# One rotation table for the S5 mixer, a weight ring opened earlier, and lane transfers moved from SyncE's queue to POOL's and ScalarE's in a hybrid decoder block

## The chip, the cores and the metric

The kernel runs on one core of a Trainium2 chip. The metric is the device time of one execution in microseconds (us). The engines are called PE (TensorE, matrix products), DVE (VectorE), ACT (ScalarE), POOL (GpSimd) and SP (SyncE, which here only issues transfers).

## The reference

One decoder block in float32, on 1024 tokens and 16 meta tokens in front of them (1040 positions), width 1024:

```python
h = LN0(concat(meta, x))
p = h @ w_in + b_in            # u_s5 512 | q 512 | k 512 | v 1024 | o 1024 | i 4 | f 4 | g_s5 1024 | g_m 1024
y_s5 = GLU(GELU(S5(u_s5)))     # per group: x_t = Abar x_{t-1} + Bbar u_t (complex, 64 states), y_t = Re(C x_t) + D u_t
y_m  = (sigmoid(o) * HeadNorm(mLSTM(q, k, v, i, f))) @ m_w_out      # 4 heads, chunkwise
mix  = sigmoid(g_s5) * y_s5 + sigmoid(g_m) * y_m
h = LN1(ALPHA * h + mix @ w_o)
h = LN2(ALPHA * h + relu(h @ w_up + b_up)**2 @ w_down)
```

The meta positions are dropped at the end.

## The kernel before, in words

**Products.** Each float32 operand of the large products is split into a rounded part ("hi", written by ACT) and a remainder ("lo", written by DVE), and each product is the sum of three matmuls (`mm3`, L226 to L228). A weight tile is loaded into `wraw`, ACT writes `whi` (L212, or L1042 in the gates), DVE writes `wlo` (L213 or L1043), and PE reads both. Some products are done by a scheme of seven half-size products in place of eight (`Seven`, and the up and down projections); it needs sums of weight blocks and of input blocks.

**Stages.** First the layer norm of h with the first q and k products in an order written out by hand. Then a list of jobs in the order of `ORDER`: `q`, `v`, `o`, `u`, `g` (g_s5), `m` (the first two of g_m), and after it eight `z` jobs (the GLU products). A job takes one weight tile through all columns of h. Then the other six tiles of g_m and m_w_out in the scheme of seven (`gates_and_output`), then w_o with LN1, the up projection and the down projection with LN2.

**Lanes.** Beside the jobs run generators, called lanes: `cv` (convolution of q and k), `ml` (gate rows and mLSTM, head after head), `s5c` (constants of the S5 mixer), `s5` (its four batches of 8 groups), `s5g` (GELU), `ah` (scaled residual and weight sums of the first three pairs of the up projection). After every two terms of a product `pump` advances an estimated clock, and each lane whose due time has come emits its next piece. The yields are these due times. The `s5` lane waits until the constants of its batch are there, and an `o` job drives the `ml` lane until its head is ready.

**Order.** The instructions so emitted pass through a scheduler that simulates the engines and fixes the order of each engine's and each queue's instructions; earlier emitted ones go first where they are ready, and weight splits have a raised priority. On the chip each queue is then in order: an instruction that waits holds all behind it. `tc.keep_in_program_order` pins some transfers to the order of emission.

**Memory.** Nearly all large tiles come from one pool of 30 slots of 128 x 1056 floats (`slot`). A tile gets its slot when the last reader of the slot's former tile has ended. Small tiles of the first stages lie in the pool `mid`. When `mid` is closed, a pool `ring` of three 128 x 1024 tiles takes its place, for the weight tiles of `gates_and_output`.

**S5.** The recurrence is run on blocks of 8 positions: 130 blocks, a real scan with decay r8 after rotation by a unit complex number p8 to the power of the block number. `s5_pre` makes Abar, its powers E, r8 and p8. `s5_consts(b)` makes for batch b the matrices Mi, RS and Mx and the table T, the cosines and sines of the powers 0 to 129 of p8 for the batch's four columns, by eight doublings of six DVE operations (`cmul`, L572 to L577) on the scratch tile `s5tt`. `s5_batch(b)` reads u from DRAM (`u_load`, L786), multiplies (tile `s5Z`), rotates, scans, rotates back, and writes y (L863). `s5_gelu(b)` reads y in another layout (`s5yc`, L871) and writes `gelh` and `gell` (L877, L878), which the z jobs read.

**Around the seam from z7 to the gates.** `begin` issues eight loads of h (`rawb`, L991), `first` then loads three weight tiles (L1024), splits the first and forms block differences. The products n = 1 and 2 use blocks of h as they lie in hT; from n = 6 on, changed blocks are written over them.

**Weight sums.** `w_sums` has POOL issue 16 transfers from DRAM to DRAM, some adding on the way, each behind a copy of one element (`mark`, L972) that waits for the weight split of the current job.

**Transfers.** All lane transfers but those into Mx and the weight sums are issued by SP, in one queue with the weight loads.

Of the kernel before, what the change touches and what calls it, by code (L numbers as in the profile page):

```python
# [40 lines left out]
ORDER = "q0 q1 v0 q2 v1 q3 o1 o0 v2 o2 o3 u0 u1 v3 u2 g0 u3 g1 o4 o5 o7 o6 g2 g3 g5 g6 g4 g7 m0 m1"  # L41
S5_START = "u0"
NM = 2
# [69 lines left out]
def decoder_block(  # L113
# [80 lines left out]
    def load_w(job):  # L194
        job.raw = []
        for src, n in job.loads:
            r = slot("wraw") if ring[0] is None else ring[0].tile([P, 1024], F32, tag="wr", bufs=3, name="wraw")
            nc.sync.dma_start(r[:, :n], src)
            job.raw.append(r)
# [111 lines left out]
    def v_job(h):  # L311
# [53 lines left out]
    def gates():  # L365
        with ExitStack() as gc:
# [43 lines left out]
            v_.tensor_tensor_scan(gg, one, a, mp, op0=OP.add, op1=OP.max)  # L410
            nc.sync.dma_start(grow_dr, gg)
            wi = gt("lf2")
            a_.activation(wi, gg, AF.Exp, scale=-1.0, bias=mp)
            nc.sync.dma_start(wrow_dr, wi)
            em = gt("fr2")
# [9 lines left out]
    def bcast_row(dst, src, h):  # L425
        nc.sync.dma_start(dst[:, 0:META], bass.AP(tensor=src.tensor, offset=src.offset + h * P,
                                                  ap=[[0, P], [1, META]]))
        nc.sync.dma_start(dst[:, META:LEN].rearrange("p (c s) -> p c s", s=P),
                          bass.AP(tensor=src.tensor, offset=src.offset + (4 + h) * P,
                                  ap=[[0, P], [4 * P, NCH - 1], [1, P]]))  # L430
# [104 lines left out]
    def u_job(i):  # L535
        st = {}

        def evac(bi, c0, c1, ps):
            if bi == 0:
                st["u"] = slot("uT")  # L540
            o = st["u"][:, :LEN].rearrange("p (j c) -> p c j", j=8)
            a_.activation(o[:, c0 // 8:c1 // 8, :], ps.rearrange("p (c j) -> p c j", j=8), AF.Identity,
                          bias=bft[:, JU + i:JU + i + 1])

        def done():
            nc.sync.dma_start(us_dr[i * P:(i + 1) * P].rearrange("p j c -> p (j c)"), st["u"][:, :LEN])
# [32 lines left out]
    def s5_pre():  # L579
        def t16(name):  # L580
            return mid.tile([P, 16], F32, name="s5_" + name)
        lam = mid.tile([P, 112], F32, tag="row", bufs=1, name="s5_lam")[:, :48].rearrange("p (a b) -> p a b", a=3)
        nc.sync.dma_start(lam, s5l)
        bc = slot("s5bc")
        nc.sync.dma_start(bc[:, 0:512], s5b)
        nc.sync.dma_start(bc[:, 512:1024], s5c)
        S5["bc"] = bc
        dtl = mid.tile([32, 16], F32, name="s5_d")
        nc.sync.dma_start(dtl, s5d)
        S5["d"] = dtl  # L590
# [72 lines left out]
        def v3(ap):  # L663
# [5 lines left out]
             v3(tm[:, 0:256]), v3(tm[:, 256:512]))  # L669
        yield 1.3  # L670

    GEL = {}

    def s5_consts(b):
# [85 lines left out]
        yield K5[b]  # L760
        T = slot("s5T")
        tc_, ts_ = (T[:, i * 520:(i + 1) * 520].rearrange("p (q c) -> p q c", q=4) for i in range(2))
        tmp = slot("s5tt")
        g_.memset(tc_[:, :, 0], 1.0)
        g_.memset(ts_[:, :, 0], 0.0)
        g_.tensor_copy(tc_[:, :, 1], S5["p8"][:, 0, q0:q0 + 4])
        g_.tensor_copy(ts_[:, :, 1], S5["p8"][:, 1, q0:q0 + 4])
        yield C5[b]
        n = 1
        while n < 129:  # L770
            m = min(n, 129 - n)
            sh = [P, 4, m]
            w1 = tmp[:, 0:4 * m].rearrange("p (q c) -> p q c", q=4)
            w2 = tmp[:, 512:512 + 4 * m].rearrange("p (q c) -> p q c", q=4)
            cmul(v_, tc_[:, :, n + 1:n + 1 + m], ts_[:, :, n + 1:n + 1 + m], tc_[:, :, 1:m + 1], ts_[:, :, 1:m + 1],
                 tc_[:, :, n:n + 1].to_broadcast(sh), ts_[:, :, n:n + 1].to_broadcast(sh), w1, w2)
            n *= 2
            yield C5[b]
        S5["m", b] = (RS, Mi, Mx, T)

    def u_load(b):
        U = slot("s5U")
        uv = U[:, :8 * NB].rearrange("p (g c) -> p g c", g=8)
        for j in range(8):
            src = us_dr[b * P:(b + 1) * P, j, :].rearrange("(g h) c -> h g c", h=16)
            nc.sync.dma_start(uv[16 * j:16 * j + 16], src)  # L786
        S5["u", b] = U
        return U

    def s5_batch(b):  # L790
# [60 lines left out]
        for hf in range(2):  # L851
# [10 lines left out]
            yield Y5[b]  # L862
        nc.sync.dma_start(ys_dr[b].rearrange("p g c -> p (g c)"), Y[:, 0:1024])  # L863
        lanes["s5g"].add(s5_gelu(b))

    def s5_gelu(b):
        yield 3.0
        yc = slot("s5yc")
        for g in range(8):
            src = ys_dr[b, :, (g % 2) * 4 + g // 2, :].rearrange("(t h) c -> h t c", h=16)  # L870
            nc.sync.dma_start(yc[16 * g:16 * g + 16, 0:1024].rearrange("p (t c) -> p t c", t=8), src)  # L871
# [6 lines left out]
        v_.tensor_tensor(lo[:, 0:1024], gf[:, 0:1024], f32(hi[:, 0:1024]), op=OP.subtract)  # L878
        GEL[b] = (hi, lo)
        yield 2.6  # L880
# [3 lines left out]
    def o_job(f):  # L884
        def evac(bi, c0, c1, ps):
            if bi == 0:
                o_job.s = slot("osig")
            a_.activation(o_job.s[:, c0:c1], ps, AF.Sigmoid, bias=bft[:, JO + f:JO + f + 1])
            v_.tensor_tensor(HM[f][:, c0:c1], HM[f][:, c0:c1], o_job.s[:, c0:c1], op=OP.mult)

        def done():
            nc.sync.dma_start(hm_dr[f], HM.pop(f)[:, :D])
        fm_job(JO + f, HALF, META, evac, done)
# [64 lines left out]
    def w_sums():  # L958
        todo = {}
        for s, (n0, p0, w, i0) in enumerate(((3, 0, wf, JGM + NM), (4, 3, wmo, 0))):  # L960
            def src(r, kh):
                return bass.AP(tensor=w.tensor, offset=w.offset + (i0 + r) * KT * P * P + 512 * kh,
                               ap=[[2 * KT * P * P, n0], [KT * P, P], [1, 512]])
            a11, a12, a21, a22 = src(0, 0), src(0, 1), src(1, 0), src(1, 1)
            d = [ws_dr[p0:p0 + n0, i] for i in range(4)]
            todo[s] = [(d[0], a21, 0), (d[2], a11, 0), (d[0], a22, 1), (d[2], a21, 1), (d[1], d[0], 0), (d[1], a11, 1),
# [37 lines left out]
    class Seven:  # L1004
# [138 lines left out]
    def gates_and_output():  # L1143
# [46 lines left out]
        return begin, first, run  # L1190

# [177 lines left out]
    def ah_scale():  # L1369
        gb = [slot("gB0"), slot("bB0")]  # L1370
        for i in range(2):
            nc.sync.dma_start(gb[i][:, :D], row_bcast(ln0r, D, i * D))
        rs = {}
        for t in range(9):
            if t < 8:
                rs[t] = slot("ahr")
                nc.sync.dma_start(rs[t][:, :D], ah0_dr[t * P:(t + 1) * P, :])
            if t == 0:
# [9 lines left out]
            nc.sync.dma_start(ah_dr[(t - 1) * P:t * P, :], r[:, :D])  # L1388

# [10 lines left out]
    def up_early():  # L1400
        for p in range(PRE):
            r = [slot("wur"), slot("wur")]
            for j in range(2):
                nc.sync.dma_start(r[j][:, :D], wup[2 * p + j].rearrange("p k f -> p (k f)"))
            yield 3.0
# [3 lines left out]
            for n, w in ((1, a11), (2, a12), (3, n2[:, 0:512]), (4, a22), (5, n1[:, 0:512]), (6, n1[:, 512:1024]),  # L1409
# [3 lines left out]
                v_.tensor_tensor(o[:, 512:1024], w, f32(o[:, 0:512]), op=OP.subtract)  # L1413
                nc.sync.dma_start(wu_dr[p, n - 1], f32(o[:, 0:1024]))
                yield 0.9
# [662 lines left out]
```

## Time and profile before

| | |
|---|---|
| median of 3 runs | 1566.78 us (1564.85 to 1566.83) |
| profiled execution | 1566.04 us, span 1564.2 us |
| mean granted clock of TensorE | 0.984 |
| busy share of the span | PE 97%, DVE 69%, ACT 41%, POOL 7% |
| DMA | 261.32 MB, mean 167 GB/s |

The span runs from the first to the last instruction. The profile has the busy time of each engine, the time an engine was idle before an instruction and what released it (a wait), and the clock that PE was granted. Times in the views are us from the start of the span. PE's share is that of the matmuls; an in-order engine that waits is idle. Names in the views are those of the program's tiles, "out<-in".

### The profile page before, as it was taken

Reading aid. Unit: us, or ns where it says so; the run is one execution under the profiler, and the core shown is the slowest. Engines: PE = TensorE matmul, PEld = TensorE weight load, DVE = VectorE, ACT = ScalarE, POOL = GpSimd, SP = SyncE. Lnnn points to the kernel's source line nnn. Section 1 sums busy time; section 2 is a strip of 40 time slices with the busy share of each in tenths; the row PEclk is TensorE's granted clock in tenths of the full one; section 3 lists DMA queues with packets and bytes.
Section 4 is the critical chain, followed back from the end, with each engine's and each line's share of the span. In section 5 each row is a group of like instructions: output and inputs, shape, how many; then the busy total and the mean of one; then the engine's idle time right before and its main releaser. Section 6 shows DMA issues by size and latency. Waiting matters only on the chain.

```text
span 1564.2 us, 20543 instructions
## 1 busy us (share of the span) xinstructions
PE 1515.8 (97%) x7593; PEld 1278.7 (82%) x7593; DVE 1079.9 (69%) x2083; ACT 642.7 (41%) x982; POOL 102.2 (7%) x195
## 2 busy tenths in 40 slices
PE   8999999998999998989999999999999999999997
PEld 8998988996878886768788887888888888888886
DVE  7667555659867845677789675666666679766786
ACT  6523353333355433325534324444444534433340
POOL 0000001124031200000000001000000000000000
PEclk9999999998999999989999999999999999999999
DMA  8412324414354556775353328644443798667642
GB/s 311 159 57 61 100 62 129 122 37 112 104 129 103 164 182 218 279 269 195 108 170 114 108 76 247 225 158 149 147 149 123 248 363 322 230 229 236 216 166 108
DMA packets 137509, 261.32 MB, mean 167 GB/s; under 512 B 30768, under 2 KB 52984, under 8 KB 137352
## 3 DMA queue, kind: packets, MB, share of 16 engines
q1 hardware_dynamic: 111344, 233.00, 43.7%
q0 software_dynamic: 26064, 27.01, 7.1%
q8 instruction: 60, 0.98, 0.3%
q14 instruction: 41, 0.34, 0.1%
HBM read 188.78 MB, written 84.55 MB: 175 GB/s over the span
## 4 chain that ended last, share of the span: by engine, by line
PE 31%; issue 23%; DMA 3%; DVE 2%; ACT 0%; SPq 0%; POOL 0%; POOLq 0%; DVEq 0%
PE mm L228 7%; PE mm L227 7%; PE mm L226 7%; PE sd L227 3%; PE sd L226 3%; PE sd L228 3%; DMA wpre<-wu_dr 1%; DMA rawb<-h_dr 1%; DMA wu_dr<-wpre 1%; DMA wur<-in_wup_dram 0%; DVE wlo L1043 0%; DVE wlo L213 0%; DMA woraw<-in_wo_dram 0%; POOL wpre L1621 0%; SPq L991 0%
## 5 line engine op out<-in xcount | busy, mean ns | idle before, releaser
L226 PE MATMUL mm<-hT_hi,whi 128*128 128x512 f32 (+3 forms) x604 | 231.0, 382 | 8.0 <-ACT whi L1042 5.4
L228 PE MATMUL mm<-hT_hi,wlo 128*128 128x512 f32 (+3 forms) x604 | 226.7, 380 | 5.7 <-DVE wlo L213 3.7
L227 PE MATMUL mm<-hT_lo,whi 128*128 128x512 f32 (+3 forms) x604 | 229.1, 379 | 0.0
L226 PEld LDWEIGHTS mm<-hT_hi,whi 128*128 128x128 f32 x604 | 115.7, 192 | 26.6 <-ACT whi L1042 6.2
L228 PEld LDWEIGHTS mm<-hT_hi,wlo 128*128 128x128 f32 x604 | 115.0, 191 | 25.5 <-DVE wlo L213 4.3
L227 PEld LDWEIGHTS mm<-hT_lo,whi 128*128 128x128 f32 x604 | 115.6, 191 | 17.6 <-issue 0.4
L227 PE MATMUL sd<-dwl,dah 128*128 128x512 f32 x240 | 94.5, 394 | 0.0
L228 PE MATMUL sd<-dwh,dal 128*128 128x512 f32 x240 | 94.4, 394 | 0.0
L226 PE MATMUL sd<-dwh,dah 128*128 128x512 f32 x240 | 94.2, 393 | 0.0
L1773 ACT ACTIVATE dah<-da 128x1024 fp32r<-128x1024 f32 x56 | 58.7, 1052 | 86.2 <-PE sd L227 38.9
L1777 ACT ACTIVATE dwh<-wdr 128x1024 fp32r<-128x1024 f32 x56 | 58.9, 1053 | 84.0 <-DMA wdr<-in_wdn_dram 27.5
L1774 DVE TENSOR_TENSOR dal<-da,dah 128x1024 fp32r<-128x1024 f32 x56 | 68.2, 1219 | 23.8 <-ACT dah L1773 23.3
L228 PE MATMUL mm<-dwh,dal 128*128 128x512 f32 (+1 forms) x224 | 84.5, 378 | 0.0
L226 PE MATMUL mm<-dwh,dah 128*128 128x512 f32 (+1 forms) x224 | 84.4, 377 | 0.0
L227 PE MATMUL mm<-dwl,dah 128*128 128x512 f32 (+1 forms) x224 | 84.3, 377 | 0.0
L1778 DVE TENSOR_TENSOR dwl<-wdr,dwh 128x1024 fp32r<-128x1024 f32 x56 | 68.2, 1219 | 13.1 <-ACT dwh L1777 12.4
L226 PE MATMUL mm<-whi,hT_hi 128*128 128x256 f32 (+1 forms) x256 | 75.2, 294 | 0.0
L228 PE MATMUL mm<-whi,hT_lo 128*128 128x256 f32 (+1 forms) x256 | 74.7, 292 | 0.0
L227 PE MATMUL mm<-wlo,hT_hi 128*128 128x256 f32 (+1 forms) x256 | 73.8, 288 | 0.0
L213 DVE TENSOR_TENSOR wlo<-wraw,whi 128x1024 fp32r<-128x1024 f32 (+1 forms) x46 | 56.1, 1222 | 19.1 <-ACT whi L212 18.6
L228 PE MATMUL mm<-th,wul 128*128 128x512 f32 x156 | 61.6, 395 | 0.0
L227 PE MATMUL mm<-tl,wuh 128*128 128x512 f32 x156 | 61.5, 394 | 0.0
(474 smaller groups left out, 3703.1 us busy)
## 6 DMA issues: line engine op xcount, KB each, us to landing
da<-act_dr SPq DMA_DIRECT2D x56, 512.0 KB, 5.4
wdr<-in_wdn_dram SPq DMA_DIRECT2D x56, 512.0 KB, 6.3
wur<-in_wup_dram SPq DMA_DIRECT2D x32, 512.0 KB, 4.3
act_dr<-upy SPq DMA_DIRECT2D x64, 256.0 KB, 2.5
wraw<-in_wf_dram SPq DMA_DIRECT2D x30, 512.0 KB, 6.9
wu_dr<-wpre SPq DMA_DIRECT2D x21, 512.0 KB, 4.7
wpre<-wu_dr POOLq DMA_DIRECT2D x21, 512.0 KB, 5.0
act_dr<-upx SPq DMA_DIRECT2D x32, 256.0 KB, 2.8
```

The source lines that it names most:

```text
L213: todo.append(lambda e=v_, r=r, hi=hi, lo=lo, n=n: e.tensor_tensor(lo[:, :n], r[:, :n], f32(hi[:, :n]), op=OP.subtract))
L226: t_.matmul(ps, ah, bh, start=(i == 0 and part[0]), stop=False, skip_group_check=skip)
L227: t_.matmul(ps, ah, bl, start=False, stop=False, skip_group_check=skip)
L228: t_.matmul(ps, al, bh, start=False, stop=(i == n - 1 and part[1]), skip_group_check=skip)
L1773: a_.activation(ah[:, :D], a[:, :D], AF.Copy)
L1774: v_.tensor_tensor(alo[:, :D], a[:, :D], f32(ah[:, :D]), op=OP.subtract)
L1777: a_.activation(wh, raw[i], AF.Copy)
L1778: v_.tensor_tensor(wl, raw[i], f32(wh), op=OP.subtract)
```

## The change

1. **One rotation table.** A new generator `s5_table` in the lane `s5c`, right behind `s5_pre`, makes the powers 0 to 65 of p8 for all 16 columns at once, in a tile of its own in `mid`, by seven rounds of `cmul`. In each batch ACT copies the batch's four columns of it into T, and one `cmul` on 4 x 64 elements makes the powers 66 to 129. `S5_START` is `o2` instead of `u0`, so `s5_pre` is emitted two jobs earlier.
2. **Ring.** `mid` is closed and the ring opened before z4 instead of z7; it has four buffers instead of three. The first three weight tiles of the gates are loaded before z6 (`early`), ahead of `begin`, instead of in `first` behind it. The jobs' own weight tiles all come from `slot`.
3. **Weight sums.** In the access patterns of the transfers of `w_sums` the 128 rows are the outermost dimension, and the 3 or 4 tiles the next.
4. **Issuers.** The transfers of bias rows, gate rows, broadcasts, S5 constants, U, yc, hm, the scaled residual and the early weight sums are issued by POOL (`g_`) instead of SP; those of wrow, u and y by ACT (`a_`).
5. The space set aside for POOL's transfer descriptors is 4096 instead of its default.

```diff
-S5_START = "u0"
+S5_START = "o2"
...
-            r = slot("wraw") if ring[0] is None else ring[0].tile([P, 1024], F32, tag="wr", bufs=3, name="wraw")
+            r = slot("wraw")
...
-            nc.sync.dma_start(bvt, row_bcast(bv, DV, h * DV))
+            g_.dma_start(bvt, row_bcast(bv, DV, h * DV))
...
-            nc.sync.dma_start(grow_dr, gg)
+            g_.dma_start(grow_dr, gg)
...
-            nc.sync.dma_start(wrow_dr, wi)
+            a_.dma_start(wrow_dr, wi)
...
-        nc.sync.dma_start(dst[:, 0:META], bass.AP(tensor=src.tensor, offset=src.offset + h * P,
+        g_.dma_start(dst[:, 0:META], bass.AP(tensor=src.tensor, offset=src.offset + h * P,
...
-            nc.sync.dma_start(us_dr[i * P:(i + 1) * P].rearrange("p j c -> p (j c)"), st["u"][:, :LEN])
+            a_.dma_start(us_dr[i * P:(i + 1) * P].rearrange("p j c -> p (j c)"), st["u"][:, :LEN])
...
+    def s5_table():
+        S5["T"] = T = mid.tile([P, 2, 16, 66], F32, name="s5_T")
+        tm, (c, s) = slot("s5tt"), (T[:, 0], T[:, 1])
+        g_.memset(c[:, :, 0], 1.0)
+        g_.memset(s[:, :, 0], 0.0)
+        g_.tensor_copy(c[:, :, 1], S5["p8"][:, 0])
+        g_.tensor_copy(s[:, :, 1], S5["p8"][:, 1])
+        yield 1.3
+        n = 1
+        while n < 65:
+            m = min(n, 65 - n)
+            sh = [P, 16, m]
+            cmul(v_, c[:, :, n + 1:n + 1 + m], s[:, :, n + 1:n + 1 + m], c[:, :, 1:m + 1], s[:, :, 1:m + 1],
+                 c[:, :, n:n + 1].to_broadcast(sh), s[:, :, n:n + 1].to_broadcast(sh),
+                 *(tm[:, i * 512:i * 512 + 16 * m].rearrange("p (q c) -> p q c", q=16) for i in range(2)))
+            n *= 2
+            yield 1.3
...
-        g_.memset(tc_[:, :, 0], 1.0)
-        g_.memset(ts_[:, :, 0], 0.0)
-        g_.tensor_copy(tc_[:, :, 1], S5["p8"][:, 0, q0:q0 + 4])
-        g_.tensor_copy(ts_[:, :, 1], S5["p8"][:, 1, q0:q0 + 4])
+        a_.activation(tc_[:, :, 0:66], t1, AF.Copy)
+        a_.activation(ts_[:, :, 0:66], s1, AF.Copy)
+        sh = [P, 4, 64]
+        cmul(v_, tc_[:, :, 66:130], ts_[:, :, 66:130], t1[:, :, 2:66], s1[:, :, 2:66],
+             t1[:, :, 64:65].to_broadcast(sh), s1[:, :, 64:65].to_broadcast(sh),
+             *(tmp[:, i * 512:i * 512 + 256].rearrange("p (q c) -> p q c", q=4) for i in range(2)))
         yield C5[b]
-        n = 1
-        while n < 129:
-            m = min(n, 129 - n)
...
-            nc.sync.dma_start(uv[16 * j:16 * j + 16], src)
+            g_.dma_start(uv[16 * j:16 * j + 16], src)
...
-        nc.sync.dma_start(ys_dr[b].rearrange("p g c -> p (g c)"), Y[:, 0:1024])
+        a_.dma_start(ys_dr[b].rearrange("p g c -> p (g c)"), Y[:, 0:1024])
...
-            nc.sync.dma_start(yc[16 * g:16 * g + 16, 0:1024].rearrange("p (t c) -> p t c", t=8), src)
+            g_.dma_start(yc[16 * g:16 * g + 16, 0:1024].rearrange("p (t c) -> p t c", t=8), src)
...
-                               ap=[[2 * KT * P * P, n0], [KT * P, P], [1, 512]])
+                               ap=[[KT * P, P], [2 * KT * P * P, n0], [1, 512]])
...
-            d = [ws_dr[p0:p0 + n0, i] for i in range(4)]
+            d = [ws_dr[p0:p0 + n0, i].rearrange("n p c -> p n c") for i in range(4)]
...
-            r = ring[0].tile([P, 1024], F32, tag="wr", bufs=3, name="wraw")
+            r = ring[0].tile([P, 1024], F32, tag="wr", bufs=4, name="wraw")
...
-        def first():
+        def early():
             for i in range(3):
                 g.load(i)
+
+        def first():
             g.split(0)
...
+            lanes["s5c"].add(s5_table())
...
-        if j.tag == "z7":
+        if j.tag == "z4":
             mid_ctx.close()
             ring_ctx = ExitStack()
             ring[0] = ring_ctx.enter_context(tc.tile_pool(name="ring", bufs=1, side="left"))
+        if j.tag == "z6":
+            early()
+        if j.tag == "z7":
             begin()
...
-    nc = _bacc.Bacc("TRN2", target_bir_lowering=False, num_devices=1)
+    nc = _bacc.Bacc("TRN2", target_bir_lowering=False, num_devices=1, dynamic_dma_scratch_size=4096)
```

In the same way as the lines shown, `g_` takes the place of `nc.sync` in the second transfer of `bcast_row`, the four of `s5_pre`, that of hm in `o_job`, and all of `ah_scale` and `up_early`.

More of the change, by code (lines that the diff above doesn't have):

```diff
@@ L425, in bcast_row @@
     def bcast_row(dst, src, h):
-        nc.sync.dma_start(dst[:, 0:META], bass.AP(tensor=src.tensor, offset=src.offset + h * P,
+        g_.dma_start(dst[:, 0:META], bass.AP(tensor=src.tensor, offset=src.offset + h * P,
                                                   ap=[[0, P], [1, META]]))
-        nc.sync.dma_start(dst[:, META:LEN].rearrange("p (c s) -> p c s", s=P),
+        g_.dma_start(dst[:, META:LEN].rearrange("p (c s) -> p c s", s=P),
                           bass.AP(tensor=src.tensor, offset=src.offset + (4 + h) * P,
@@ L582, in s5_pre @@
         lam = mid.tile([P, 112], F32, tag="row", bufs=1, name="s5_lam")[:, :48].rearrange("p (a b) -> p a b", a=3)
-        nc.sync.dma_start(lam, s5l)
+        g_.dma_start(lam, s5l)
         bc = slot("s5bc")
-        nc.sync.dma_start(bc[:, 0:512], s5b)
-        nc.sync.dma_start(bc[:, 512:1024], s5c)
+        g_.dma_start(bc[:, 0:512], s5b)
+        g_.dma_start(bc[:, 512:1024], s5c)
         S5["bc"] = bc
         dtl = mid.tile([32, 16], F32, name="s5_d")
-        nc.sync.dma_start(dtl, s5d)
+        g_.dma_start(dtl, s5d)
         S5["d"] = dtl
@@ L760, in s5_consts @@
         yield K5[b]
-        T = slot("s5T")
+        T, tmp = slot("s5T"), slot("s5tt")
+        t1, s1 = S5["T"][:, 0, q0:q0 + 4], S5["T"][:, 1, q0:q0 + 4]
         tc_, ts_ = (T[:, i * 520:(i + 1) * 520].rearrange("p (q c) -> p q c", q=4) for i in range(2))
-        tmp = slot("s5tt")
-        g_.memset(tc_[:, :, 0], 1.0)
-        g_.memset(ts_[:, :, 0], 0.0)
-        g_.tensor_copy(tc_[:, :, 1], S5["p8"][:, 0, q0:q0 + 4])
-        g_.tensor_copy(ts_[:, :, 1], S5["p8"][:, 1, q0:q0 + 4])
-        yield C5[b]
-        n = 1
-        while n < 129:
-            m = min(n, 129 - n)
[L772 to L778, printed above, removed]
+        a_.activation(tc_[:, :, 0:66], t1, AF.Copy)
[4 more added lines that the diff above has]
+             *(tmp[:, i * 512:i * 512 + 256].rearrange("p (q c) -> p q c", q=4) for i in range(2)))
+        yield C5[b]
         S5["m", b] = (RS, Mi, Mx, T)
@@ L891, in done @@
         def done():
-            nc.sync.dma_start(hm_dr[f], HM.pop(f)[:, :D])
+            g_.dma_start(hm_dr[f], HM.pop(f)[:, :D])
         fm_job(JO + f, HALF, META, evac, done)
@@ L1189, in run @@
             y.run(lambda c, p: sdps() if c == "b" and p else mmps(), ym_evac, yhooks)
-        return begin, first, run
+        return early, begin, first, run
     def ln0_load(t):
@@ L1371, in ah_scale @@
         for i in range(2):
-            nc.sync.dma_start(gb[i][:, :D], row_bcast(ln0r, D, i * D))
+            g_.dma_start(gb[i][:, :D], row_bcast(ln0r, D, i * D))
         rs = {}
@@ L1376, in ah_scale @@
                 rs[t] = slot("ahr")
-                nc.sync.dma_start(rs[t][:, :D], ah0_dr[t * P:(t + 1) * P, :])
+                g_.dma_start(rs[t][:, :D], ah0_dr[t * P:(t + 1) * P, :])
             if t == 0:
@@ L1387, in ah_scale @@
                 yield 1.5
-            nc.sync.dma_start(ah_dr[(t - 1) * P:t * P, :], r[:, :D])
+            g_.dma_start(ah_dr[(t - 1) * P:t * P, :], r[:, :D])
     wu_dr = dram.tile([PRE, 7, P, 1024], F32, name="wu_dr")
@@ L1403, in up_early @@
             for j in range(2):
-                nc.sync.dma_start(r[j][:, :D], wup[2 * p + j].rearrange("p k f -> p (k f)"))
+                g_.dma_start(r[j][:, :D], wup[2 * p + j].rearrange("p k f -> p (k f)"))
             yield 3.0
@@ L1413, in up_early @@
                 v_.tensor_tensor(o[:, 512:1024], w, f32(o[:, 0:512]), op=OP.subtract)
-                nc.sync.dma_start(wu_dr[p, n - 1], f32(o[:, 0:1024]))
+                g_.dma_start(wu_dr[p, n - 1], f32(o[:, 0:1024]))
                 yield 0.9
@@ L1467, in decoder_block @@
     next(ws)
-    begin, first, run7 = gates_and_output()
+    early, begin, first, run7 = gates_and_output()
     for i, j in enumerate(jobs):
```

## The prediction

> **What bounds the kernel now.** I read the head of the page first, then PE's share by stretches, then the list of what PE waited for. The first fence has lines of the page; the second is the view of stretches, whose columns are the length, the busy time of PE, PE's weight loads, DVE, ACT and POOL with their instruction counts, and the granted clock, DMA share and GB/s.
>
> ```profile
> span 1564.2 us, 20543 instructions
> ...
> PE 1515.8 (97%) x7593; PEld 1278.7 (82%) x7593; DVE 1079.9 (69%) x2083; ACT 642.7 (41%) x982; POOL 102.2 (7%) x195
> ```
>
> ```profile
> 340.00:390.00 50.00, 40.64 (x217) 35.49 (x216) 44.41 (x154) 18.86 (x36) 18.16 (x20) 0.86 0.35 98
> ...
> 590.00:612.00 22.00, 16.72 (x59) 12.78 (x58) 14.59 (x14) 6.63 (x9) 2.08 (x2) 0.84 0.74 242
> 612.00:685.00 73.00, 70.07 (x298) 55.10 (x297) 42.97 (x63) 25.33 (x40) 0.00 (x0) 1.00 0.74 262
> 685.00:705.00 20.00, 12.70 (x44) 9.40 (x43) 15.93 (x16) 4.74 (x6) 0.00 (x0) 0.74 0.62 222
> 705.00:1555.00 850.00, 849.61 (x3745) 691.54 (x3744) 610.53 (x883) 354.45 (x529) 11.20 (x21) 1.00 0.55 187
> ```
>
> The reader is to see that PE is the bound and that its matmuls are not touched. From 705 us to 1555 PE is idle for 0.39 us of 850 at full clock. So all that the change can win is PE's idle time before 705 and the clock that dropped with it. Three stretches hold most of it. Their idle is length minus busy: 9.36 us in 340:390, 5.28 in 590:612, 7.30 in 685:705. Between them, 612:685 has 2.93; what lies earlier I leave as it is. The clock adds to this: (1 - 0.86) x 50 = 7.0 us of clock in the first, 0.16 x 22 = 3.5 in the second, 0.26 x 20 = 5.2 in the third. Idle that fell inside the slow time would be counted twice: off A's clock goes half of 3.7 + 1.1, the waits after the clock fell there, and off C's half of 5 of its 7.3 us. That leaves 4.6, 3.5 and 2.7. I call the stretches A, B and C. A is worth 14.0 us, B 8.8, C 10.0; together 32.8. What PE waited for in A, in B and in C, each from the list of waits in that stretch:
>
> ```profile
> PE mm L228 <- DVE wlo L213: 3.7, 1, 3.7
> PE s5k L741 <- DVE s5Ri L719: 2.9, 1, 2.9
> PE mm L226 <- DVE v L354: 1.3, 1, 1.3
> PE mm L226 <- ACT whi L212: 1.1, 1, 1.1
> ```
>
> ```profile
> PE mm L227 <- DVE gell L878: 3.1, 1, 3.1
> PE mm L226 <- DVE z2s L944: 2.1, 1, 2.1
> ```
>
> ```profile
> PE mm L226 <- ACT whi L1042: 5.4, 1, 5.4
> PE mm L228 <- DVE wlo L1043: 1.9, 1, 1.9
> ```
>
> The reader is to see that DVE, not a DMA, is the last to arrive in A and B, and a late weight tile in C. Gaps of 2.1 and 3.1 us in B brought the clock to 0.84. [...]
>
> **Part 1: one rotation table, begun at o2.** A is short of DVE. The DVE's busy time by stretches, and that of the instructions on the table's scratch tile (s5tt) alone:
>
> ```profile
> 260.00:300.00 40.00, 23.20 (x84) 1.00 0.40 124
> 300.00:340.00 40.00, 24.98 (x79) 1.00 0.27 59
> 340.00:380.00 40.00, 35.04 (x117) 0.93 0.35 103
> 380.00:420.00 40.00, 36.52 (x103) 0.90 0.38 107
> ```
>
> ```profile
> 340.00:420.00 80.00, 18.95 (x96) 0.91 0.36 105
> ...
> sum 200.00, DVE 37.86; mean DVE 12.62
> ```
>
> ```profile
> L572 DVE TENSOR_TENSOR s5tt<-s5T x32: 147/180/426, 346.6 to 524.5; 128x4 f32<-128x4 f32 x8, 128x8 f32<-128x8 f32 x4, 128x16 f32<-128x16 f32 x4, 128x32 f32<-128x32 f32 x4
> ```
>
> ```profile
> L838 DVE TENSOR_TENSOR s5Z<-s5w,s5T x4: 665/669/680, 378.9 to 543.4; 128x512 f32<-128x512 f32 x4
> ```
>
> Before, each of four batches builds its table in 8 doublings of 6 operations: 37.86 / 4 = 9.5 us. The two rows on single lines give durations in ns, least/median/most, and the forms: the doublings run from 4 elements, 0.147 us, to 256, 0.426 us; 512 elements take 0.669. After, a batch has one complex product of 6 operations on 4 x 64 = 256 elements: 6 x 0.426 = 2.6 us. The shared table is 7 rounds of 6 operations, on 16, 32, 64, 128, 256, 512 and again 16 elements. Its rounds of 16 to 256 are those of a batch now, 9.5 less three rounds of 4, 4 and 8 elements at 6 x 0.147 = 0.9, so 6.8; the round of 512 adds 6 x 0.669 = 4.0 and the last about 1.0: 11.8 us, once. DVE does 37.9 us before and 4 x 2.6 + 11.8 = 22.2 after. What counts is where. In 340:420 two tables of 18.95 us shrink to 5.2, so DVE falls from 35.04 + 36.52 = 71.6 of 80 us to about 58. The 11.8 go ahead of it, where DVE is busy 23.20 and 24.98 of 40. If they all fell into 260:300 it would stand at 35.0, as full as 340:380 is now; so part of the wait can come back there. ACT gets 8 copies of 264 elements, POOL loses 14 of its 16 small ones; neither bounds A. I take three quarters of A, 10.5 us (ends 0 and 14.0). Late next is the fourth head's chain of small DVE operations, which the change leaves where it is.
>
> **Part 2: the sooner and deeper ring.** C is an order in SP's queue:
>
> ```profile
> 673.55 3.02 SPq L1414 DMA_DIRECT2D wu_dr<-wpre  x3
> 676.63 6.08 SPq L991 DMA_DIRECT2D rawb<-h_dr  x8
> 682.75 6.99 SPq L1024 DMA_DIRECT2D wraw<-in_wf_dram  x6
> ```
>
> The first three weight tiles of the gates (L1024) are issued after eight loads of h (L991), which stand behind the stores of up_early (L1414). Only from there come whi L1042 and wlo L1043, for which PE waits 5.4 and 1.9 us. After, the ring is open at z4 and the tiles are loaded at z6, two jobs ahead, with four buffers; the L1414 stores leave SP. The products n = 1 and 2 read what already lies in hT, so nothing else holds PE at the seam; the first changed block is wanted two products later. I take 9 of C's 10.0 (ends 7 and 10). Late next are the subtractions on rawb (L1002).
>
> **Part 3: lane transfers on POOL and ACT.** Counted in the code, 142 transfers go from SP to POOL: bias rows 4, grow 1, gB and wiB 16, constants 4, U 32, yc 32, hm 8, ah_scale 18, up_early 27. Nine go to ACT. On SP they stood in one queue with the weight loads and with each other, as in this row of SP's waits:
>
> ```profile
> SPq L871 <- DMA ah_dr<-ahr: 7.5, 1, 7.5
> ```
>
> This is B: the last of eight loads of yc for batch 3 waited 7.5 us for a store of ah_scale, and gell, for which PE waits, hangs on that load. With batch 3 sooner by what the tables gave back (its own table took 9.5 us of DVE) and the ah lane begun where it was, the 3.1 us of PE's wait need only part of that. I take 7 of B's 8.8 (ends 0 and 8.8). Of the 2.93 us in 612:685 I take 2, since the weight loads there stand behind the stores of L1414; ends 0 and 2.9.
>
> What POOL pays, from its timeline and from the issues of the weight sums (ns, least/median/most):
>
> ```profile
> 373.94 6.26 POOL L766 COPY s5T<-s_p 128x4 f32<-128x4 f32 x1
> 380.15 3.06 POOL L767 COPY s5T<-s_p 128x4 f32<-128x4 f32 x1
> 383.14 4.06 POOL L758 DMA_DIRECT2D s5Mx<-s5Kt  x8
> ```
>
> ```profile
> L974 POOL DMA_DIRECT2D ws_dr<-in_wmo_dram x6: 1129/1650/1963, 267.7 to 602.1; - x6
> ```
>
> An issue costs POOL 4.06 / 8 = 0.51 us, a large one up to 1.96: 142 x 0.51 = 72 to 142 x 1.96 = 278 us, spread over most of the first 700, on an engine with 102.2 us of work. It holds that, but its queue is in order: bvt waits there for the last head's additions, the stores of ah_scale and up_early for DVE, the marks of the weight sums for whi; behind them stand gB, U and yc, for which DVE and then PE wait. I take 2 us for these, and 2 us for the table's DVE work ahead of A; ends 0 and, for POOL, far more (below). ACT's nine issues wait for ACT's own results: nothing.
>
> **Part 4: weight sums with rows outermost.** The last is issued at 602.1 us and the first is read after the loads at 682.75; no PE wait above hangs on them. Nothing, ends -1 and 1.
>
> **The sum.** 10.5 + 9 + 7 + 2 - 2 - 2 = 24.5 us. The profiled execution took 1566.04 us, 1.84 more than its span; less 24.5 that is 1541.5. It lies 0.7 under the median of the runs, 1566.78, so against the median I say 1542.
>
> **The rivals.** *Only the seam is won* (0.20). The batches are not sooner because their tiles wait for slots, and the table's 11.8 us make a new stretch like A before 340. For it speaks this row, a weight load that waited 31.6 us in SP for a slot:
>
> ```profile
> SPq L198 <- PE pS L463: 31.6, 1, 31.6
> ```
>
> Against it: the table's relief inside 340:420 needs no slot. C's 9 remain and 1 to 3 of the rest: 1566.8 - 11 = 1556, 1550 to 1563.
>
> *POOL becomes late* (0.13), the side slower than before. Two copies of 4 elements took 6.26 and 3.06 us on POOL while DVE was full, and all lane transfers would stand behind such instructions. A transfer late by 6.3 us stops PE for that long and takes some 1.7 us of clock, as each of B's two gaps did (3.5 / 2): 8 us. There are 12 places: gB for 4 heads, U and yc for 4 batches. From 24.5 / 8, so 3 of the 12, the gain is gone; at 5 it is 1542 + 40 = 1582. Against it: the 8 issues from 383.14 on took 0.51 us each just after those copies, in a stretch in which DVE was busy 36.52 of 40 us. [...]
>
> *Nothing is left of it* (0.07): the new waits eat the gain and the time stays at 1564 to 1570. [...]
>
> **How the numbers follow.** The forecast has 0.57: from 1531 (A, B, C and all of 612:685, 32.8 + 2.9 off 1566.8) to 1552. The other 0.03 lie below. The range over all runs from 1529 to 1565, with the forecast, the seam alone and the near half of no change inside. 0.2% is 3.1 us and about what a measurement tells from no change. Faster holds the forecast, what lies below and the seam: 0.80; the last case and the edge of the seam's give 0.07 within; slower 0.13.
>
> **What would show it.** Part 1: the fourth-head stretch without 3.7 and 2.9 us waits, and DVE near 58 of 80. Part 2: no wait on whi L1042 at the start of the gates, whose tiles are loaded ahead of rawb. Part 3: no wait on gell; POOL's issues about 0.5 to 2 us. I am wrong if PE's waits turn up on gB, kw or s5z instead, if POOL is busy over half of the first 700 us, or if something opens after 705.

## The result, and the profile after

The changed kernel takes 1569.37 us in the median (1567.89 to 1573.65), the kernel before 1566.78 (1563.54 to 1568.31). The ratio is 1.0024, 95% interval 1.0012 to 1.0035: no gain, a loss of about 0.2%. The profiled execution is the slowest of the nine, 1573.65 us, so the traces lie further apart (7.7 us of span) than the medians. The forecast was 1542, with a range of 1529 to 1565 and 0.80 on faster.

First the busy times from the page of the changed kernel, whose span is 1571.9 us, then its stretches with the columns used before:

```profile
PE 1521.0 (97%) x7593; PEld 1283.0 (82%) x7593; DVE 1063.7 (68%) x1957; ACT 645.6 (41%) x990; POOL 163.4 (10%) x325
```

```profile
340.00:390.00 50.00, 42.75 (x250) 38.30 (x250) 33.20 (x83) 21.92 (x45) 21.54 (x40) 0.93 0.48 122
390.00:450.00 60.00, 51.81 (x253) 41.89 (x252) 45.81 (x98) 26.69 (x49) 21.94 (x41) 0.92 0.41 107
450.00:560.00 110.00, 98.07 (x427) 77.84 (x426) 47.41 (x121) 45.49 (x67) 28.76 (x49) 0.87 0.40 106
590.00:612.00 22.00, 22.00 (x97) 17.89 (x96) 10.76 (x9) 3.70 (x5) 3.74 (x7) 1.00 0.72 262
612.00:685.00 73.00, 69.01 (x295) 55.79 (x294) 41.71 (x60) 23.98 (x37) 13.74 (x25) 0.98 0.68 231
685.00:705.00 20.00, 20.00 (x86) 16.19 (x85) 12.11 (x16) 5.55 (x8) 2.75 (x6) 0.97 1.01 373
705.00:1555.00 850.00, 847.35 (x3709) 688.52 (x3708) 620.24 (x893) 357.81 (x533) 11.16 (x21) 1.00 0.55 188
```

The same view of the kernel before, for the two stretches that the prediction did not show:

```profile
340.00:450.00 110.00, 100.64 (x535) 86.67 (x534) 86.56 (x265) 46.46 (x82) 29.06 (x41) 0.94 0.39 107
450.00:560.00 110.00, 105.94 (x525) 86.75 (x524) 82.26 (x231) 51.58 (x80) 22.63 (x39) 1.00 0.51 136
```

The reader is to see that PE no longer stops in B (590 to 612) and C (685 to 705), as forecast: it is busy 22.00 of 22 and 20.00 of 20. Part of C has only moved: after 705 PE is now idle 2.65 us, where it was 0.39, and the prediction had named a gap after 705 as a sign of being wrong. All that was won, and more, was lost between 340 and 560. In 450:560 PE was idle 4.06 us at clock 1.00; now it is idle 11.93 at 0.87, which is 11.9 + 0.13 x 110 = 26.2 us. In 340:450 the loss goes from 9.4 + 0.06 x 110 = 16.0 us to 15.4 + 0.07 x 50 + 0.08 x 60 = 23.7.

For seven kernels of this study, here is the same account made from their traces: PE's idle time in a stretch, from its first instruction to its last, plus half of the time in which the granted clock was 0.5, both in us. Idle time that falls into such slow time counts in both.

| stretch | before | after | rows only | table, rows | table, rows, ring | the same, issuers moved | the same, start at o2 |
|---|---|---|---|---|---|---|---|
| 0:110 | 8.8 | 10.8 | 9.2 | 8.8 | 9.9 | 11.6 | 9.2 |
| 110:340 | 6.9 | 0.0 | 1.5 | 1.1 | 0.9 | 0.0 | 1.1 |
| 340:450 | 16.2 | 23.6 | 17.4 | 6.5 | 5.9 | 8.6 | 17.0 |
| 450:560 | 4.1 | 25.8 | 4.0 | 17.3 | 16.6 | 20.6 | 17.0 |
| 560:660 | 11.3 | 0.0 | 0.0 | 0.0 | 0.0 | 0.0 | 0.0 |
| 660:760 | 12.7 | 8.0 | 10.2 | 9.3 | 3.4 | 4.4 | 5.2 |
| from 760 | 4.3 | 4.0 | 3.7 | 3.6 | 2.9 | 4.1 | 3.9 |
| span | 1564.2 | 1571.9 | 1545.2 | 1546.5 | 1542.8 | 1553.5 | 1552.9 |

What PE waited for longest in the changed kernel, in 340:450 and in 450:560:

```profile
PE mm L228 <- DVE wlo L213: 5.9, 2, 3.9
PE mm L226 <- ACT whi L212: 5.6, 2, 3.4
```

```profile
PE pn L473 <- ACT kw L460: 3.5, 1, 3.5
PE s5z L812 <- DVE s5Z L820: 2.0, 1, 2.0
PE pt L513 <- DVE hraw L506: 1.7, 1, 1.7
```

The waits on kw and s5z are the ones that the prediction named as signs of being wrong. But DVE has less to do in 340:420, as forecast:

```profile
340.00:380.00 40.00, 28.14 (x71) 0.91 0.38 100
380.00:420.00 40.00, 24.08 (x54) 0.96 0.52 145
```

It is busy 52.2 of 80 us (forecast about 58, before 71.6), and PE waits more. Another named sign, POOL busy over half of the first 700 us, did not come: it is busy 163.4 us in all. ACT's timeline in the changed kernel shows one of the new waits; ACT_TABLE_LOAD there is an instruction of ACT's own and has nothing to do with the rotation table:

```profile
462.61 1.28 ACT L884 ACT_TABLE_LOAD   x1
463.90 2.08 ACT L884 ACTIVATE gelf<-s5yc 128x1024 f32<-128x1024 f32 x1
465.79 0.42 ACT L496 ACTIVATE hraw<-pn,dd 128x256 f32<-128x256 f32 x1
466.11 1.05 ACT L887 ACTIVATE gelh<-gelf 128x1024 fp32r<-128x1024 f32 x1
467.18 1.28 ACT L898 ACT_TABLE_LOAD   x1
468.47 1.27 ACT L898 ACTIVATE osig<-mm,bft 128x512 f32<-128x512 f32 x2
469.63 0.42 ACT L782 ACTIVATE s5T<-s_T 128x264 f32<-128x264 f32 x1
469.94 0.42 ACT L783 ACTIVATE s5T<-s_T 128x264 f32<-128x264 f32 x1
470.26 0.37 ACT L460 ACTIVATE kw<-pk,gB 128x128 f32<-128x128 f32 x1
```

The fourth head's kw stands behind a GELU of S5, two table loads, a sigmoid, and two of the copies that the change itself gave to ACT (L782, L783). PE has no job product to fill the time: from 467.2 to 486.5 us it runs the head's chain alone. Before, most of the same steps lay among job products, and the chain ran alone only from 459.1 to 467.5.

### The profile page after: what moved, and what is told of

It reads as the page before. It is cut to its first block, busy times and chain, and to the rows that moved or that the text cites. A ratio compares the mean times of both kernels' runs of the same rounds, so it can differ in the third digit from the quotient of the medians.

```text
span 1571.9 us, 20409 instructions
## 1 busy us (share of the span) xinstructions
PE 1521.0 (97%) x7593; PEld 1283.0 (82%) x7593; DVE 1063.7 (68%) x1957; ACT 645.6 (41%) x990; POOL 163.4 (10%) x325
## 4 chain that ended last, share of the span: by engine, by line
PE 60%; issue 25%; DVE 6%; DMA 4%; ACT 3%; POOL 1%; POOLq 0%; SPq 0%; DVEq 0%; ACTq 0%
PE mm L228 14%; PE mm L226 14%; PE mm L227 14%; PE sd L227 3%; PE sd L226 3%; PE sd L228 3%; PE mm L1317 2%; DMA wur<-in_wup_dram 1%; PE mm L1325 1%; DMA wpre<-wu_dr 1%; PE pn L473 1%; PE pn L474 1%; PE pu L477 1%; DVE rawb L1012 1%; PE ln L1273 0%
## 5 line engine op out<-in xcount | busy, mean ns | idle before, releaser
L226 PEld LDWEIGHTS mm<-hT_hi,whi 128*128 128x128 f32 x604 | 116.3, 193 | 26.2 <-ACT whi L212 7.9
L1790 DVE TENSOR_TENSOR dal<-da,dah 128x1024 fp32r<-128x1024 f32 x56 | 68.1, 1219 | 24.1 <-ACT dah L1789 23.7
L228 PE MATMUL mm<-whi,hT_lo 128*128 128x256 f32 (+1 forms) x256 | 73.1, 285 | 0.0
```

Source lines behind the costliest of these rows:

```text
L226: t_.matmul(ps, ah, bh, start=(i == 0 and part[0]), stop=False, skip_group_check=skip)
L228: t_.matmul(ps, al, bh, start=False, stop=(i == n - 1 and part[1]), skip_group_check=skip)
L1790: v_.tensor_tensor(alo[:, :D], a[:, :D], f32(ah[:, :D]), op=OP.subtract)
```

## The experiments

Ratios are against the kernel before, run beside each on the same chip, with 95% intervals.

| kernel | median us | ratio | interval |
|---|---|---|---|
| ring | 1561.32 | 0.9983 | 0.9974 to 0.9992 |
| table, rows | 1547.72 | 0.9893 | 0.9878 to 0.9908 |
| issuers, old rows | 1627.71 | 1.0405 | 1.0385 to 1.0424 |
| issuers, rows | 1553.34 | 0.9921 | 0.9909 to 0.9934 |
| rows | 1545.76 | 0.9874 | 0.9861 to 0.9887 |
| rows, old descriptor space | 1548.71 | 0.9890 | 0.9873 to 0.9906 |
| table, rows, ring | 1544.21 | 0.9863 | 0.9850 to 0.9876 |
| table, rows, ring, issuers | 1554.94 | 0.9937 | 0.9922 to 0.9952 |
| table, rows, ring, o2 | 1554.50 | 0.9932 | 0.9919 to 0.9945 |
| rows, ring | 1541.76 | 0.9848 | 0.9830 to 0.9867 |
| rows, ring, o2 | 1550.24 | 0.9907 | 0.9891 to 0.9922 |
| rows, ring, 33 slots | 1540.05 | 0.9841 | 0.9825 to 0.9858 |
| rows, ring, 33 slots, o2 | 1548.04 | 0.9890 | 0.9872 to 0.9908 |
| rows, ring, gate issuers | 1539.94 | 0.9838 | 0.9823 to 0.9853 |
| rows, ring, S5 issuers | 1550.71 | 0.9904 | 0.9889 to 0.9919 |
| rows, ring, late issuers | 1545.57 | 0.9870 | 0.9855 to 0.9886 |
| rows, ring, u and y on ACT | 1541.21 | 0.9845 | 0.9832 to 0.9859 |
| rows, ring, 33 slots, gate issuers | 1540.75 | 0.9842 | 0.9828 to 0.9855 |

**One part at a time.** Four kernels: before with the ring alone, with the table (and the row order), with the issuers alone, and the changed kernel begun at u0.

```diff
 # ring alone
-        if j.tag == "z7":
+        if j.tag == "z4":
             mid_ctx.close()
...
+        if j.tag == "z6":
+            early()
 # changed kernel, S5 from u0
-S5_START = "o2"
+S5_START = "u0"
```

> The kernel before with the ring part alone (ring opened at z4, four buffers, tiles loaded at z6). Theory E (the changed kernel lost in 340 to 560 us, because the sooner S5 start crowds the fourth head's chain; the seam was won all the same): the seam's 9 to 10 us come free of any loss, 1555 to 1559. Rival (the seam's gain shows only because the transfers left SP's queue, the ring alone moves the tiles behind the same stores): 1563 to 1567, with a wait of over 3 us still on whi of the gates.

> The kernel before with the shared table, the weight sums' row order and the smaller descriptor space, S5 still begun at u0, all lane transfers still on SP. Theory E: the table by itself does no harm and relieves DVE in 340 to 420, 1558 to 1566. Rival T (the table itself is the harm: its work delays the first batch, or the copies on ACT stand in the heads' way): 1568 to 1575, with the new gaps of 350, 440 and 467 us in place.

> The kernel before with the lane transfers issued by POOL and ACT, nothing else. Theory E: the queue of POOL is not what PE waits for, 1556 to 1566, the wait on gell gone. Rival P (POOL late, as in my prediction): 1570 to 1585, with PE's waits on kw, s5z and v grown.

> The changed kernel with S5 begun at u0 again, all else as changed. Theory E: the loss in 340 to 560 goes with the sooner start, so 1545 to 1556. Rivals P and T: the loss stays, 1566 to 1572.

Ring alone gives 1561.3, between the two expectations: a gain, a third of the forecast one. The table run gives 1547.7, far faster than any theory said; the changed kernel begun at u0 gives 1554.9 instead of 1569.4, so the sooner start does harm. The issuers alone cost 63 us, far more than either theory said. In their trace the order of POOL's queue stands out. POOL's timeline, then the waits of DVE and of PE in 300:340:

```profile
296.43 1.44 POOL L974 DMA_DIRECT2D ws_dr<-in_wf_dram  x1
297.58 3.99 POOL L786 DMA_DIRECT2D s5U<-us_dr  x7
324.20 0.54 POOL L786 DMA_DIRECT2D s5U<-us_dr  x1 [22.64 <-DMA ws_dr<-in_wf_dram]
324.73 0.96 POOL L645 COPY s5E<-s5E 128x32 f32<-128x32 f32 x6
```

```profile
DVE s5tm L696 <- POOL s5E L645: 18.7, 1, 18.7
```

```profile
PE pS L463 <- DVE C L482: 16.2, 1, 16.2
```

The eighth load of U waits 22.64 us until a weight sum has landed, with which it shares no data: seven issues stand between them, and the same count of seven stands before the waits of 12.9 and 15.0 us at 477 and 550 us. Why it is seven the traces do not show. Behind it stand POOL's six small copies, behind these DVE, behind DVE the third head's chain and PE.

**The row order.** If so, sums that land sooner should cure it. The next kernels are the issuers with rows outermost, the row order alone, and two more combinations.

```diff
-                               ap=[[2 * KT * P * P, n0], [KT * P, P], [1, 512]])
+                               ap=[[KT * P, P], [2 * KT * P * P, n0], [1, 512]])
...
-            d = [ws_dr[p0:p0 + n0, i] for i in range(4)]
+            d = [ws_dr[p0:p0 + n0, i].rearrange("n p c -> p n c") for i in range(4)]
```

> The kernel before with the lane transfers on POOL and ACT and the weight sums with rows outermost (and the smaller descriptor space), no table, old ring, S5 from u0. Theory L (on POOL a transfer waits until the one eight before it has landed; with the old sums, 25 to 28 us to landing, the eighth load of U waited 22.6 us, a load of yc 12.9, one of U 15.0, and DVE and PE stood behind POOL's copies; with rows outermost the sums land in 5 to 12 us): 1565 to 1582, the waits of POOL on ws_dr each under 6 us, no PE wait of over 5 us at 311 and 470. Rival Q (POOL's queue is late behind the stores of hm, the scaled residual and the early weight sums, whatever the sums take): over 1600.

> The kernel before with rows outermost in the weight sums and the smaller descriptor space alone. My prediction priced this at nothing: 1563 to 1566 against 1564.3. Theory L, in which the transfers into s5Mx on POOL waited 16.9 us for a sum too: some of the 16.6 us of the table run came from here, 1555 to 1562.

> Table, rows outermost and ring, S5 from u0, all lane transfers on SP. If the parts add (table run -16.6, ring run -3.0): 1542 to 1548, faster than both kernels. If the ring's gain was the same stall as the table's: 1547 to 1550.

> The changed kernel with all lane transfers back on SP; table, rows, ring and the start at o2 stay. Theory E (the sooner start is harmful by itself, since the batches then fall on the fourth head's chain and on ACT's weight splits): 1553 to 1562, some 10 over the same without the sooner start. Rival (the sooner start is harmful only with POOL as issuer): within 3 us of the kernel with table and ring and S5 from u0, 1542 to 1549.

With rows outermost the issuers' run falls from 1627.7 to 1553.3, more than theory L had expected, and Q falls. POOL's timeline at the same place:

```profile
291.82 0.79 POOL L974 DMA_DIRECT2D ws_dr<-in_wf_dram  x1
292.60 3.74 POOL L786 DMA_DIRECT2D s5U<-us_dr  x7
300.19 0.53 POOL L786 DMA_DIRECT2D s5U<-us_dr  x1 [3.85 <-DMA ws_dr<-in_wf_dram]
```

The wait is 3.85 us instead of 22.64. But the row order also gives 20 us without any new issuer: 1545.8, below both expectations and as much as the table run, in which it was contained. Why, these rows show. First the kernel before: the DMA issues (size, median us to landing), POOL's queue on the page, the DMA engines' busy tenths from 615 to 637 us, while a sum issued at 602 is under way to 637, and from 560:612 DVE's longest wait and the stretch itself, with the time to landing of all yc loads:

```profile
ws_dr<-in_wmo_dram POOLq DMA_DIRECT2D x6, 1024.0 KB, 29.1
ws_dr<-in_wf_dram POOLq DMA_DIRECT2D x6, 768.0 KB, 26.3
```

```profile
q0 software_dynamic: 26064, 27.01, 7.1%
```

```profile
DMA  8999999632222222222222399996222222222599
```

```profile
DVE ahr L1386 <- DMA ahr<-ah_dr: 27.0, 4, 14.8
```

```profile
DMA to landing us min/median/max: 2.4/7.4/14.2
```

```profile
560.00:612.00 52.00, 46.72 (x191) 37.23 (x190) 24.15 (x22) 14.62 (x17) 2.84 (x4) 0.93 0.65 215
```

And the kernel with the row order (and the smaller descriptor space) alone:

```profile
ws_dr<-in_wmo_dram POOLq DMA_DIRECT2D x6, 1024.0 KB, 8.8
ws_dr<-in_wf_dram POOLq DMA_DIRECT2D x6, 768.0 KB, 7.2
```

```profile
q0 software_dynamic: 10704, 26.88, 7.2%
```

```profile
DVE ahr L1386 <- DMA ahr<-ah_dr: 5.6, 2, 4.0
```

```profile
DMA to landing us min/median/max: 2.3/4.6/7.6
```

```profile
560.00:612.00 52.00, 52.00 (x226) 42.25 (x225) 26.99 (x30) 18.62 (x23) 1.45 (x2) 1.00 0.75 235
```

The old sum keeps the DMA engines busy at two tenths for long stretches. Of 16 engines that is about 3, near the size of the outermost dimension, 3 or 4. With 128 rows outermost it lands in 7 to 9 us instead of 26 to 29. What else is in flight lands sooner: yc in 4.6 us in the median, not 7.4; DVE waits 5.6 us for the scaled residual's loads, not 27.0; and gell is there when PE wants it. The 5.4 us before 340 come the same way. While a sum issued at 104.2 us was under way, the 24 KB of `s_lam`, the first of S5's constants, took 5.6 us to land, and DVE stood for them. In the changed kernel, where the sum issued at 105.9 had landed in 5.0 us before they were issued at 113.4, they took 2.6. DVE's wait in the kernel before:

```profile
DVE s_t L557 <- DMA s_lam<-in_s5l_dram: 3.6, 1, 3.6
```

In the changed kernel this wait is 0.9 us, and PE's wait of 2.0 us for gts at 124.8 is gone, as it is with the rows alone. So B, and the 5.4 us, came from the sums, not from SP's queue. A rival is that POOL's own loads into s5Mx, which waited 16.9 us for sums before, gave the gain; those waits end at 459 and 520 us, and the account of 340:560 is no better with the rows alone.

The share of the engines that POOL's queue had busy is 17.8% of 16, or 2.8, from 615 to 637 us, against 54.0%, or 8.6, from 594 to 606 with the row order. Why the share goes with the order, no run shows. POOL's queue also has fewer packets in all, 10704 for 26064, for about the same bytes, 26.88 and 27.01 MB. The sum issued at 602 shows the share of each. The small packets come first: 844 packets for 0.03 MB from 602 to 606. From 615 to 637 there are 356 packets for 0.72 MB, 2 KB each, the size that the kernel with the row order has too (528 for 1.05 MB). So in these 22 of its 35 us the sum was slow with packets of the same size and fewer engines busy; no run changes one of the two alone.

**Where the sooner start hurts.** The last two combinations differ in `S5_START` alone: 1544.2 from u0, 1554.5 from o2. Theory E holds in that the harm needs no new issuer. One row of the kernel with o2, from ACT's waits in 430:450, spoke for slots as its cause:

```profile
ACT whi L212 <- DVE s5Ri L737: 4.2, 1, 4.2
```

whi shares no data with L737, only the slot of a tile that L737 read last. The next four kernels test this without the table.

```diff
-    big = ctx.enter_context(tc.tile_pool(name="big", bufs=30, side="left"))
+    big = ctx.enter_context(tc.tile_pool(name="big", bufs=33, side="left"))
```

> Rows outermost and ring alone, S5 from u0, old tables, all lane transfers on SP. If rows (-19.7) and ring (-3.0) add and the table is worth nothing: 1541 to 1544, as fast as the kernel with table, rows and ring (1544.2) or faster. If the table is worth its 15.7 us of DVE work: 1548 or more.

> The same with S5 begun at o2. In the kernel with the table the sooner start cost some 10 us (1554.5 against 1544.2). Both theories of its cause (S, slots: S5's tiles hold slots that the weight splits and the heads wait for; E, order: the batches' DVE and ACT work falls on the fourth head's chain whatever the slots) expect 1550 to 1558 here. If only table and start together harm: 1541 to 1546.

> Rows outermost and ring, S5 from u0, with 33 slots in the large pool instead of 30. Theory S: some slots were missing even here, 1536 to 1542. Theory E: 1541 to 1545, no change.

> Rows outermost and ring, S5 begun at o2, 33 slots. Theory S: the harm of the sooner start goes, within 3 us of the same kernel with S5 from u0 and 33 slots, and the wait of whi on a slot last read by L719 is gone. Theory E: 7 us or more remain between the two.

The start at o2 costs 8.5 us with 30 slots and 8.0 with 33, so theory S falls: slots are not the cause. (In these two traces with o2 whi waited for no slot, even with 30.) And the kernel without the table is not slower, 1541.8 against 1544.2. What the table does, its stretches show (table and rows):

```profile
340.00:450.00 110.00, 105.17 (x569) 90.21 (x567) 85.38 (x201) 56.58 (x109) 32.81 (x60) 0.98 0.43 121
450.00:560.00 110.00, 101.21 (x467) 83.35 (x468) 57.52 (x118) 51.59 (x68) 17.43 (x27) 0.92 0.48 130
```

340:450 is relieved, PE busy 105.17 us instead of 100.64 before, and the next stretch pays it back, 101.21 at clock 0.92 instead of 105.94 at 1.00: in the account above 10.9 us less, then 13.3 more, than with the rows alone. There PE's longest waits, 7.1 us in two, are for hraw of the fourth head's chain. The start at o2 without the table (rows and ring, 30 slots) shows something else. Its stretches, then PE's longest waits in 340:560:

```profile
340.00:450.00 110.00, 99.29 (x513) 84.03 (x512) 80.77 (x247) 45.58 (x81) 23.10 (x49) 0.95 0.43 124
450.00:560.00 110.00, 104.91 (x498) 85.22 (x497) 76.08 (x201) 49.30 (x77) 17.38 (x30) 0.95 0.48 119
```

```profile
PE mm L226 <- ACT whi L212: 4.9, 4, 2.1
PE mm L228 <- DVE wlo L213: 4.3, 3, 2.3
PE pn L473 <- ACT s5Y L861: 2.5, 1, 2.5
```

In the same two stretches of the same kernel begun at u0, PE is busy 100.65 and 105.92 us at clock 0.94 and 1.00. So its idle time rises only from 13.4 to 15.8 us. More is lost to the clock: four spells of 3.4 us at half clock become six, 6.8 us of loss become 10.2. The stops of over 0.5 us are nine instead of six, the longest 2.5 us instead of 3.7, and they are strewn more widely: at u0 all four slow spells lie between 365 and 385 us, at o2 they begin near 355, 375, 425, 460 and, two of them, 510. That the batches fall on the fourth head's chain and on the weight splits is read from these traces; no run moved the batches alone, so this part of theory E is argued, not shown.

**Which issuers cost.** On the kernel with rows and ring, one group of transfers was moved at a time, and as a control the row order was tried with the old descriptor space.

```diff
 # gate: bias rows, grow, gB, wiB to POOL, wrow to ACT
-            nc.sync.dma_start(bvt, row_bcast(bv, DV, h * DV))
+            g_.dma_start(bvt, row_bcast(bv, DV, h * DV))
 # S5: constants, U, yc to POOL, u and y to ACT
-            nc.sync.dma_start(uv[16 * j:16 * j + 16], src)
+            g_.dma_start(uv[16 * j:16 * j + 16], src)
 # late: hm, scaled residual, early weight sums to POOL
-            nc.sync.dma_start(hm_dr[f], HM.pop(f)[:, :D])
+            g_.dma_start(hm_dr[f], HM.pop(f)[:, :D])
```

> Rows and ring (1541.8), and of the issuers only bias rows, grow and the broadcasts gB and wiB to POOL, wrow to ACT. Theory Q (POOL's order: a transfer that waits for DVE holds the small copies and memsets of S5 behind it; bvt waits there up to 23.3 us): 1543 to 1548. Theory D (a transfer on POOL costs by its own, in the spread of the DMA work; then the groups with most transfers cost most, U and yc and the early sums): 1540 to 1543 here.

> Rows and ring, and of the issuers only S5's: constants, U and yc to POOL, u and y to ACT. Theory Q (U and yc wait in POOL's queue, in turn with the weight sums and the transfers into s5Mx): 1545 to 1552, new waits in 340 to 560 us. Theory D: 1544 to 1550 too, but with no wait of POOL over 5 us. If these are free: 1540 to 1543.

> Rows and ring, and of the issuers only hm, the scaled residual and the early weight sums to POOL. Theory Q: the stores wait on POOL for DVE (58.3 and 58.9 us in all in the run with issuers alone), and the weight sums of the gates stand behind them; the seam at 670 to 700 us pays, 1544 to 1550. If it frees SP for the weight loads, as my prediction had it: 1536 to 1541.

> The kernel before with rows outermost in the weight sums and nothing else, the descriptor space as before. If the row order alone brings the gain: 1544 to 1548, as with the smaller space (1545.8). If the space had part in it: 1550 or more.

Only S5's group costs beyond the intervals, 1550.7 against 1541.8. The gate group is free (1539.9). The late group's 1545.6 lies above, with overlapping intervals. This settles neither theory: Q had 1543 to 1548 for the gate group, and D had no wait of POOL over 5 us for S5's, where a load of yc waited 6.3 us for the store of y. The row order with the old space is 1548.7, so the order brings the gain and the space at most a small part.

> Rows and ring, and of S5's transfers only the stores of u and y issued by ACT. If the loads on POOL pay (they wait there in turn with the weight sums and stand before POOL's memsets and copies): 1540 to 1543. If ACT pays (a store waits in ACT's own order, and ACT writes whi and kw behind it): 1548 to 1552.

With only the stores of u and y on ACT it is 1541.2: ACT's issues cost nothing that can be measured here, and POOL's loads of constants, U and yc pay. In the trace of S5's group no single long stop stands out; 450:560 goes from 4.1 to 10.3 us in the account, which is all of the 6.0 us by which the spans of the two profiled executions differ (1548.1 and 1542.1). The medians differ by 8.9.

**A version that beats both.**

> Rows, ring, 33 slots, bias rows and gate rows issued by POOL and ACT; S5 from u0, old tables, all else on SP. If the small gains add (slots -1.7, gate group -1.8 on 1541.8): 1537 to 1540; if they were noise: 1540 to 1543. In either case some 24 us under the kernel before.

It takes 1540.8, 1.6% under the kernel before and as fast as rows and ring alone within the intervals. Two lines of access patterns and the ring do it; more slots and the gate issuers add nothing that can be measured.

## Why the prediction was wrong

The forecast was 24.5 us faster, and the kernel is 2.6 slower. Three parts failed on the way there: part 1, where I charged nothing for the fourth head's chain and counted the sooner start as help; part 3, where I credited the issuers with 7 us; and part 2, whose size was too large. The largest error, part 4, went the other way and hid most of this.

**Part 4.** I priced the row order at 0, ends -1 and 1, because the sums are not needed before the gates. It is worth 17 to 20 us. I asked who waits for a sum and not what else is in flight beside it; the two rows with 26.3 and 29.1 us to landing were in the trace of before.

**Part 3.** The 7 us of B were won, but not by the issuers: with the row order alone the stretch is already free, so that this sign came true was luck. SP's wait of 7.5 us on the store of ah_dr, on which I built the term, was itself, by the rows above, a transfer held up; with the rows alone it is 2.8 us. The issuers cost: 7.6 us on the rows (1553.3 less 1545.8) and 10.7 with table and ring, where I had +2 for POOL. The rival of a late POOL had the right mechanism, an in-order queue, and the wrong places: not the transfers that PE's data come by, but small copies standing behind them, and a wait on the transfer eight issues back. It is large only with the old sums, 22.64 us against 3.85 with the rows. Moving an issue won nothing that these runs can tell: on rows and ring, 1541.8 us, the gate group gave 1539.9, u and y on ACT 1541.2, the late group 1545.6 and S5's 1550.7.

**Part 1.** Begun at u0, the table gives 340:450 its 10.9 us, against a forecast of 10.5 for A. DVE's relief was smaller than worked out: with table and rows it is busy 63.5 of 80 us in 340:420, against 73.1 with the rows alone, so 9.6 us less where I had 13.8. That the changed kernel shows 52.2, near my 58, is luck: the sooner start had moved work of the batches out of this stretch, as it does without the table (63.2). What failed is the line "Late next is the fourth head's chain of small DVE operations, which the change leaves where it is": I named it and charged nothing. It took back 13.3 us. The sooner start, which I counted as help, costs 8 to 10 more. A small slip beside it, on which nothing hangs: POOL loses 16 small operations and gets 4 new ones, so 12 less and not 14.

**Part 2.** Right in its mechanism, the tiles are there before the loads of h and the 5.4 us wait is gone; its size was 3 to 4 us, not 9. With the ring alone the tiles are issued at 676.2 us instead of 682.8, since they still stand behind stores of up_early, as the rival expectation had it, and PE's wait for wlo grows from 1.9 to 5.1 us. On the rows alone PE still waited at the seam for whi and wlo, and with the ring it waits for wlo alone, the second fence:

```profile
PE mm L226 <- ACT whi L1042: 3.1, 1, 3.1
PE mm L228 <- DVE wlo L1043: 1.9, 1, 1.9
```

```profile
PE mm L228 <- DVE wlo L1043: 3.4, 2, 2.0
```

The stretch 612:685, forecast 2 us better, has 3.99 us of idle time instead of 2.93, one wait for wlo.

**The sum by the runs.** Table, rows and ring together 1544.2; the sooner start +10.3, the issuers +10.7: 1565.2. The changed kernel is some 4 us above that. The kernel before itself ran at 1564.3 to 1566.8 us beside these runs, which were on several chips, so 1 to 2 us of it can come from there. In the account the two losses together exceed their sum in 340:450 (23.6 us, where 5.9 + 11.1 + 2.7 make 19.7) and in 450:560 (25.8, where 16.6 + 0.4 + 4.0 make 21.0). What they meet in there is open.

## What to carry to other kernels

The sums, for which no stop of PE had waited, were not free here, 17 to 20 us: look at how long a transfer takes to land and what lands beside it, and try the long dimension outermost, which took 29.1 us to landing down to 8.8. DVE's relief was worth only what the next chain let through, 10.9 us won and 13.3 paid back, so that chain needs a price of its own. Before moving issues to another engine's queue, list the small work of that engine that will stand behind them: here six copies stood behind a wait of 22.64 us, and DVE behind them for 18.7.

## What the runs showed of the hardware

The median time to landing of the same 1024 KB was 29.1 us before and 8.8 us with the 128 rows outermost and the smaller descriptor space. With the old descriptor space the row order gave 1548.7 us, against 1545.8; the time to landing is not shown for it. Beside a slow transfer a load of 24 KB took 5.6 us, and 2.6 in the changed kernel, where none was under way. And a short gap was followed by a slow clock: in the kernel with the rows alone a gap of 1.31 us at 340.3 us was followed, from 342.6 on, by 3.4 us at half clock (0.51 granted in 342.5:346), while one of 1.69 us at 457.8 was not (1.00 in 455:461), so of these two gaps it was not the longer one. In the kernel before, gaps of 3.15 and 2.13 us that ended at 598.7 and 606.1 us were each followed by half clock, 0.50 granted in 599.3:602.6 and 606.2:609.4.
